# Two-layer Fourier, retention and attention trunk on one core: the Fourier projections use four banks in turn, and the last two tiles of the output projection take a shorter residual path

## The chip, the cores and the metric

One Trainium2 chip, one of its cores. The metric is the device time of one execution in microseconds, from runs of the whole program. Engines are named as in the profile: PE is TensorE, DVE VectorE, ACT ScalarE, POOL GpSimd, and SP SyncE, which here issues the DMAs.

## The reference

Two layers of a mixer over 1152 tokens of width 1024: 128 context tokens and 1024 latent tokens, modulated by two conditioning vectors. Cut to what matters here, one layer is:

```
h   = rms_norm(x, g_pre) * (1 + scale) + shift
fx, fz, rq, rk, rv, rz, aq, ak, av, az, mg = split_columns(h @ w_in)
ya  = (fourier_mix(fx) @ w_four) * silu(fz)          # real part of a 2-D DFT
yb  = rms_norm(bidir_retention(rope(rq), rope(rk), rv)) * silu(rz)
yc  = windowed_attention(rope(aq), rope(ak), av) * silu(az)
merged = ga * (ya @ w_pa) + gb * (yb @ w_pb) + gc * (yc @ w_pc)
x   = x + gate * rms_norm(merged @ w_out, g_post)
```

All of it is in float32. Outputs are x of the second layer and, for each layer, the new keys, values and retention states of the context tokens.

## The kernel before

The tokens lie in nine tiles of 128: tile 0 is the context, tiles 1 to 8 are latent. For products over token columns they are also taken as three chunks of 384. Each float32 operand is split into a high and a low half (`hi`, `lo`; for h the arrays `HH` and `HL`), and each product is three matrix multiplications: high by high, low by high, high by low. A weight is loaded to a tile `raw` (512 KB), cast to its high half by ACT (L174) and subtracted to its low half by POOL (L175).

PSUM has eight banks, given out by name: two `pj`, two `sl`, two `tr`, one `sc`, one `pv`. A projection needs a bank until its reader has copied the result out. `proj_t` (L218 to L220) multiplies eight blocks of a transposed weight with a chunk, 24 multiplications of 384 columns. `proj_n` (L228 to L230) multiplies a token tile with 512 columns, 24 multiplications as well.

In each layer the parts come in this order:

- a first group of natural projections (retention's keys and values), one tile at a time into a `pj` bank. Tile 0 is copied by ACT (L525) to `ns`; latent tiles go through the rotary step on DVE (L482 to L492) and a copy on ACT (L539). The rope table is loaded ahead of it (L508).
- the Fourier block. For each chunk it makes four projections into `acc` (L640). Of the first two ACT casts `XH` (L643) and DVE subtracts `XL` (L644); the other two go through a gate (ACT tanh L235, DVE L237). Then the group transforms (L651 to L653) into `sl`, copied by ACT to `Pn` (L654), a butterfly over the latent tiles on DVE (L673, L677, L681), and last the products with the DFT table (L717, L730). A second group of natural projections is mixed with the butterfly; its keys and values go through `kv` (ACT L537).
- retention, attention, gates and the branches' merge.
- the output projection (the loop from L1205). Each tile is multiplied with `w_out`, half into a `pj` bank and half into `sl`. ACT takes the sum of squares of each half (L1219), DVE and POOL make the reciprocal root (L246, L248), DVE scales both halves with it and with the gate (L1239), POOL adds the old x (L1242), and x is stored (L1246).
- in layer 0 each such tile at once becomes the next layer's h in `make_h` (L259): norm (ACT Square L254, DVE L246, POOL L248, DVE L256), eight transposes on PE (L268) into two `tr` banks, four affine steps on DVE for each bank (L272), the cast to `HH` on ACT (L277) and the subtraction to `HL` on DVE (L278).

The last tile of the last layer has its own way in the program before: the products with the gate are made first (L1226, L1229), so that after the reciprocal root only one step for each half remains (L1232), and there is no sum on POOL.

In the code tokens and engines are plain loops; a scheduler places every instruction on its engine with a model of time, and each engine then works its list in order. Tiles of a pool are reused when the last reader of the place is done. So the next layer's first group is mixed with the output projection's last tiles, and a change in one place moves instructions elsewhere. Constants of the next layer are also made there: decays and masks of retention (`la` to `lg`, `RD`, `WR`, `DD`, L570 to L609), the Fourier weight `MF` (PE L628, ACT L630), and slices of the next modulation (`macc`, L435 and L437).

Of the kernel before, what the change touches and what calls it, by code (L numbers as in the profile page):

```python
# [11 lines left out]
AF = mybir.ActivationFunctionType  # L12
# [4 lines left out]
P = 128  # L17
D = 1024
KT = 8
NT = 9  # L20
TOK = NT * P
CH = 384
# [60 lines left out]
def hybrid_step(ctx, tc, ins, cst, outs):  # L83
    nc = tc.nc
    PE, ACT, DVE, POOL, SP = nc.tensor, nc.scalar, nc.vector, nc.gpsimd, nc.sync
# [26 lines left out]
    x_d = dram("scr_x", (TOK, D))  # L112
# [17 lines left out]
    def pj(shape):  # L130
        return bank("pj", 2, shape)
# [17 lines left out]
    sh = mk(const, [P, KT, 2], "sh")  # L149
    sm = mk(const, [P, KT, 2], "sm")  # L150
    siluc = mk(const, [P, KT, 2], "siluc")
    shn = mk(const, [P, KT, 2], "shn")
    smn = mk(const, [P, KT, 2], "smn")
# [102 lines left out]
        DVE.tensor_scalar(xh, xt, r, None, op0=ALU.mult)  # L256
        return xh

    def make_h(pl, xt, t, sm, sh):  # L259

        s = 0 if t == 0 else 1
        xh = norm_x(pl, xt)
        tok = slice(t * P, (t + 1) * P)
        for half in range(2):
            pt = tr([P, 4, P])
            for kk in range(4):
                k = half * 4 + kk
                PE.transpose(pt[:, kk, :], xh[:, k * P : (k + 1) * P], ident)  # L268
            hf = mk(pl, [P, 4, P], "hf")
            for kk in range(4):  # L270
                k = half * 4 + kk
                DVE.tensor_scalar(  # L272
                    hf[:, kk, :], pt[:, kk, :], sm[:, k, s : s + 1], sh[:, k, s : s + 1],
                    op0=ALU.mult, op1=ALU.add,
                )
            ks = slice(half * 4, half * 4 + 4)
            ACT.copy(HH[:, ks, tok], hf)  # L277
            DVE.tensor_tensor(out=HL[:, ks, tok], in0=hf, in1=f(HH[:, ks, tok]), op=ALU.subtract)  # L278
# [216 lines left out]
    for l in range(DEPTH):  # L495
        last = l == DEPTH - 1
# [118 lines left out]
        with pool("fo", side="right") as fo:  # L615
            gz = mk(fo, [P, 2, TOK], "gz")
            Pn = mk(fo, [P, NT, 512], "Pn")
            with pool("xt", side="right") as xp:
                MFh = mk(xp, [P, 2, 512], "MFh", F32R)
                MFl = mk(xp, [P, 2, 512], "MFl", F32R)  # L620
                cdft = mk(xp, [P, 2, P], "cdft")
                SP.dma_start(cdft, cst["cdft"].rearrange("p (a b) -> p a b", a=2))
                w4 = mk(xp, [P, 2, 256], "w4")
                SP.dma_start(w4, ins["w_four"][l].rearrange("(k p) f -> p k f", p=P))
                for i in range(2):
                    mf = sl([P, 2, 256])
                    for r in range(2):
                        PE.matmul(mf[:, r, :], cdft[:, r, :], w4[:, i, :], start=True, stop=True)  # L628
                    mfv = MFh[:, i, :].rearrange("p (a b) -> p a b", a=2)
                    ACT.copy(mfv, mf)  # L630
                    DVE.tensor_tensor(
                        out=MFl[:, i, :].rearrange("p (a b) -> p a b", a=2), in0=mf, in1=f(mfv), op=ALU.subtract
                    )
                XH = mk(xp, [P, 2, TOK], "XH", F32R)
                XL = mk(xp, [P, 2, TOK], "XL", F32R)
                us = [unit_t(w_in, c0) for c0 in (C_FX, C_FX + P, C_FZ, C_FZ + P)]
                for c in range(NCH):
                    tok = slice(c * CH, (c + 1) * CH)
                    for i in range(4):
                        acc = pj([P, CH])  # L640
                        proj_t(us[i], c, acc)
                        if i < 2:
                            ACT.copy(XH[:, i, tok], acc)  # L643
                            DVE.tensor_tensor(out=XL[:, i, tok], in0=acc, in1=f(XH[:, i, tok]), op=ALU.subtract)  # L644
                        else:
                            gate_evac(fo, acc, gz[:, i - 2, tok])
                for t in range(NT):
                    tok = slice(t * P, (t + 1) * P)
                    acc = sl([P, 512])
                    for i in range(2):  # L650
                        PE.matmul(acc, XH[:, i, tok], MFh[:, i, :], start=(i == 0), stop=False)  # L651
                        PE.matmul(acc, XH[:, i, tok], MFl[:, i, :], start=False, stop=False)
                        PE.matmul(acc, XL[:, i, tok], MFh[:, i, :], start=False, stop=(i == 1))  # L653
                    ACT.copy(Pn[:, t, :], acc)  # L654
# [550 lines left out]
        for t in range(NT):  # L1205
# [14 lines left out]
                accs.append(acc)  # L1220
            s1 = mk(wo3, [P, 1], "s1", bufs=2)
            DVE.tensor_tensor(out=s1, in0=ss[:, 0:1], in1=ss[:, 1:2], op=ALU.add)
            end = last and t == NT - 1
            if end:
                xg = mk(wo3, [P, D], "xg")
                DVE.tensor_tensor(out=xg[:, 0:512], in0=accs[0], in1=gpb[:, s, 0:512], op=ALU.mult)  # L1226
# [1 line left out]
            if end:  # L1228
                DVE.tensor_tensor(out=xg[:, 512:D], in0=accs[1], in1=gpb[:, s, 512:D], op=ALU.mult)  # L1229
                for n in range(2):  # L1230
                    ns = slice(n * 512, n * 512 + 512)
                    DVE.scalar_tensor_tensor(  # L1232
                        out=xo[:, ns], in0=xg[:, ns], scalar=r, in1=xo[:, ns], op0=ALU.mult, op1=ALU.add
                    )
                    SP.dma_start(y_s[0, (t - 1) * P : t * P, ns], xo[:, ns])
                continue
            for n in range(2):
                ns = slice(n * 512, n * 512 + 512)
# [40 lines left out]
```

## Time and profile before

| what | value |
|---|---|
| median of 3 runs | 2003.23 us (2001.77 to 2006.81) |
| the profiled execution's own time | 2004.05 us |
| its span, first to last instruction | 2002.3 us |
| PE busy | 1961.0 us, 98% |
| DVE busy | 991.0 us, 49% |
| ACT busy | 678.1 us, 34% |
| POOL busy | 549.0 us, 27% |
| mean granted PE clock | 0.995 of full speed |

Busy time is summed over the span. PE's lead over the others is so large that the idle time of any other engine costs something only where PE waits for it; the list of PE's waits and the windows in which PE is busy for less than their length are the places to look at. The granted clock of 1.00 is 2.4 GHz, 0.50 is 1.2 GHz.

### The profile page before, as it was taken

What the parts mean: (1) busy time and instruction counts of PE and PEld (TensorE: products, weight loads), DVE (VectorE), ACT (ScalarE), POOL (GpSimd) and SP (SyncE); (2) the same over time, 40 slices, a digit from 0 to 9 for tenths busy, and PEclk for the clock granted to TensorE, in tenths of its full rate; (3) what the DMA queues carried; (4) which work ended last, traced back from release to release, by engine and by line L of the source; (5) the groups of instructions that cost most, each with busy time, mean ns of one, the idle gap of its engine ahead of it and who ended that gap; (6) DMA issues with size and microseconds to landing.
All of it is one profiled execution on the core that took longest, in us unless ns stands there. A gap on an engine that the chain in (4) does not pass through costs nothing.

```text
span 2002.3 us, 29865 instructions
## 1 busy us (share of the span) xinstructions
PE 1961.0 (98%) x11046; PEld 1794.2 (90%) x11046; DVE 991.0 (49%) x2557; ACT 678.1 (34%) x1536; POOL 549.0 (27%) x424
## 2 busy tenths in 40 slices
PE   8999999999999999999999999999999999999998
PEld 2898878999999999999878878899999999999987
DVE  4626556556667765104675272444556665410411
ACT  3522111234555444114331212022455555421411
POOL 2222232111112332444441214122111222333342
PEclk9999999999999999999999999999999999999999
DMA  9323554353334334323344145234422433422142
GB/s 298 105 72 98 149 139 135 102 178 105 97 116 123 117 103 137 91 89 128 116 135 101 58 103 162 74 115 129 125 82 88 121 100 97 143 92 83 60 153 85
DMA packets 245186, 230.53 MB, mean 115 GB/s; under 512 B 37920, under 2 KB 215856, under 8 KB 244784
## 3 DMA queue, kind: packets, MB, share of 16 engines
q1 hardware_dynamic: 245040, 228.62, 37.6%
q8 instruction: 87, 1.43, 0.3%
q14 instruction: 59, 0.48, 0.1%
HBM read 170.14 MB, written 58.42 MB: 114 GB/s over the span
## 4 chain that ended last, share of the span: by engine, by line
PE 88%; DMA 4%; DVE 3%; ACT 1%; issue 1%; SPq 1%; POOL 1%; DVEq 0%; POOLq 0%; ACTq 0%
PE pj L218 13%; PE pj L220 13%; PE pj L219 13%; PE pj L228 5%; PE pj L229 5%; PE pj L230 5%; PE tr L1102 3%; DMA raw<-in_w_in 2%; PE sl L1048 2%; PE pv L1109 2%; PE pv L1108 2%; PE sl L951 2%; PE sl L953 2%; PE sl L952 2%; PE pj L951 2%; PE pj L952 2%
## 5 line engine op out<-in xcount | busy, mean ns | idle before, releaser
L218 PE MATMUL pj<-HH,uh 128*128 128x384 f32 x1440 | 491.0, 341 | 9.0 <-DVE XL L644 4.2
L219 PE MATMUL pj<-HL,uh 128*128 128x384 f32 x1440 | 485.4, 337 | 0.0
L220 PE MATMUL pj<-HH,ul 128*128 128x384 f32 x1440 | 485.3, 337 | 0.0
L175 POOL TENSOR_TENSOR ul<-raw,uh 128x1024 fp32r<-128x1024 f32 x80 | 192.4, 2406 | 491.1 <-ACT uh L174 400.0
L218 PEld LDWEIGHTS pj<-HH,uh 128*128 128x128 f32 x1440 | 271.0, 188 | 14.2 <-ACT mth L948 4.9
L219 PEld LDWEIGHTS pj<-HL,uh 128*128 128x128 f32 x1440 | 271.2, 188 | 1.6
L220 PEld LDWEIGHTS pj<-HH,ul 128*128 128x128 f32 x1440 | 270.9, 188 | 1.5
L174 ACT CAST uh<-raw 128x1024 fp32r<-128x1024 f32 x80 | 84.0, 1049 | 172.3 <-PE pj L219 123.6
L437 DVE SCALAR_TENSOR_TENSOR macc<-mw,siluc,macc 128x256 f32<-128x256 f32 x224 | 134.7, 644 | 8.2 <-DMA mw<-in_w_mod 8.2
L228 PE MATMUL pj<-uh,HH 128*128 128x512 f32 x336 | 133.7, 399 | 3.7 <-ACT kv L537 1.8
L229 PE MATMUL pj<-ul,HH 128*128 128x512 f32 x336 | 132.8, 395 | 0.0
L230 PE MATMUL pj<-uh,HL 128*128 128x512 f32 x336 | 132.3, 394 | 0.0
L954 DVE SCALAR_TENSOR_TENSOR M<-M,sl 128x384 f32<-128x384 f32 x48 | 26.6, 554 | 202.2 <-PE sl L953 197.1
L1085 ACT ACTIVATE E<-E,NM 128x640 f32<-128x640 f32 (+1 forms) x128 | 101.9, 798 | 66.5 <-DVE NM L1081 66.4
L1106 DVE TENSOR_TENSOR El<-tr,Eh 128x512 fp32r<-128x512 f32 x132 | 89.0, 685 | 45.9 <-ACT Eh L1105 45.6
L1105 ACT CAST Eh<-tr 128x512 fp32r<-128x512 f32 x132 | 74.7, 587 | 86.8 <-PE tr L1102 85.1
L966 POOL TENSOR_TENSOR mth<-mth,ml 128x384 f32<-128x384 f32 x48 | 51.7, 1077 | 178.0 <-DVE mth L954 122.5
L1102 PE MATMUL tr<-ident,E 128*128 128x128 f32 x528 | 84.0, 272 | 0.2 <-ACT E L1085 0.2
L954 DVE SCALAR_TENSOR_TENSOR mth<-mth,pj 128x384 f32<-128x384 f32 x96 | 52.9, 551 | 63.1 <-ACT mth L948 31.9
L966 POOL TENSOR_TENSOR M<-M,mrow 128x384 f32<-128x384 f32 x48 | 48.7, 1015 | 123.1 <-DVE M L954 73.5
L1066 DVE CUSTOM_DVE_ANT_0 E<-sl,mask,m 128x384 f32<-128x384 f32 (+1 forms) x128 | 72.1, 579 | 17.4 <-PE sl L1048 17.0
L228 PEld LDWEIGHTS pj<-uh,HH 128*128 128x128 f32 x336 | 63.3, 188 | 19.2 <-ACT kv L537 1.9
(312 smaller groups left out, 4038.4 us busy)
## 6 DMA issues: line engine op xcount, KB each, us to landing
raw<-in_w_in SPq DMA_DIRECT2D x84, 512.0 KB
scr_m<-mth SPq DMA_DIRECT2D x96, 192.0 KB
mw<-in_w_mod SPq DMA_DIRECT2D x128, 128.0 KB
scr_n<-ns SPq DMA_DIRECT2D x36, 256.0 KB
ml<-scr_m SPq DMA_DIRECT2D x48, 192.0 KB
mrow<-scr_m SPq DMA_DIRECT2D x16, 576.0 KB
big<-in_w_mod SPq DMA_DIRECT2D x16, 512.0 KB
raw<-in_w_out SPq DMA_DIRECT2D x16, 512.0 KB
```

The source lines that it names most:

```text
L175: POOL.tensor_tensor(out=lo, in0=raw, in1=f(hi), op=ALU.subtract)
L218: PE.matmul(acc, hi[:, k, :], HH[:, k, tok], start=(k == 0), stop=False)
L219: PE.matmul(acc, hi[:, k, :], HL[:, k, tok], start=False, stop=False)
L220: i = PE.matmul(acc, lo[:, k, :], HH[:, k, tok], start=False, stop=(k == KT - 1))
L228: PE.matmul(acc, a, hi[:, k % 2, :], start=(k == 0), stop=False)
L229: PE.matmul(acc, a, lo[:, k % 2, :], start=False, stop=False)
L230: i = PE.matmul(acc, b, hi[:, k % 2, :], start=False, stop=(k == KT - 1))
L437: DVE.scalar_tensor_tensor(out=accs[s], in0=w, scalar=siluc[:, k, s : s + 1], in1=accs[s], op0=ALU.mult, op1=ALU.add,)
L966: POOL.tensor_tensor(out=th, in0=th, in1=ml, op=ALU.add)
L1085: ACT.activation(Es[hh][:, 0:nk], srcs[hh], AF.Exp, bias=NM[t][:, hs + hh : hs + hh + 1], scale=0.125, accum_out=DEN[t][:, hs + hh : hs + ...
L1102: PE.transpose(pt[:, hh, hp_, :], Es[2 * hp_ + hh][:, n * P : (n + 1) * P], ident)
L1106: DVE.tensor_tensor(out=El, in0=pt, in1=f(Eh), op=ALU.subtract)
```

## The change

There are three edits. The four projections of a chunk in the Fourier block take the banks `pj`, `sc`, `pj` and `pv` in turn, instead of the two `pj` alone. The path without POOL's sum is taken by tiles 7 and 8 in both layers, instead of tile 8 of the last layer alone; in layer 0 its end is the store of x and `make_h`. In that call of `make_h` the second and fourth affine step of each half are done by ACT instead of DVE.

```
-    def make_h(pl, xt, t, sm, sh):
+    def make_h(pl, xt, t, sm, sh, both=False):
...
             for kk in range(4):
                 k = half * 4 + kk
+                if both and kk % 2:
+                    ACT.activation(
+                        hf[:, kk, :], pt[:, kk, :], AF.Identity, bias=sh[:, k, s : s + 1], scale=sm[:, k, s : s + 1]
+                    )
+                    continue
                 DVE.tensor_scalar(
...
-                        acc = pj([P, CH])
+                        acc = (pj, sc, pj, pv)[i]([P, CH])
                         proj_t(us[i], c, acc)
...
-            end = last and t == NT - 1
+            end = t >= NT - 2
             if end:
                 xg = mk(wo3, [P, D], "xg")
...
-                    SP.dma_start(y_s[0, (t - 1) * P : t * P, ns], xo[:, ns])
+                    if last:
+                        SP.dma_start(y_s[0, (t - 1) * P : t * P, ns], xo[:, ns])
+                if not last:
+                    SP.dma_start(x_d[t * P : (t + 1) * P, :], xo)
+                    make_h(wo3, xo, t, smn, shn, True)
                 continue
```

Line numbers in the text are those of the kernel before; in the changed kernel those of the Fourier block stand 5 further on. The order changes at the Fourier block of each layer and at the turn between the layers. Three places follow, as each engine's list has them; a number behind a name is a buffer's.

ACT's list at the start of layer 1's Fourier block, before: `XH` are the casts of the first two projections, `gth` the gates of the other two, and the second weight cast is for a later stage.

```order
L174 CAST uh_10817<-raw_10815 128x1024
L643 CAST XH_10795<-pj_10821 128x384
L174 CAST uh_11262<-raw_11259 128x1024
L643 CAST XH_10795<-pj_10848 128x384
L235 ACTIVATE gth_10900<-pj_10875 128x384
L235 ACTIVATE gth_10934<-pj_10909 128x384
```

And with the change:

```order
L174 CAST uh_10821<-raw_10819 128x1024
L648 CAST XH_10799<-pj_10825 128x384
L174 CAST uh_11266<-raw_11263 128x1024
L648 CAST XH_10799<-sc_10852 128x384
L235 ACTIVATE gth_10904<-pj_10879 128x384
L235 ACTIVATE gth_10938<-pv_10913 128x384
```

The order on ACT is the same, with the same weight cast between the two `XH`; only the banks that are read differ.

ACT's list at the turn from layer 0 to layer 1, before: L277 are casts of tile 7's halves, L525 the copy of tile 0 of the next layer's first projection out of its bank, L254 tile 8's Square.

```order
L572 ACTIVATE lu_10724<-la_10722 128x8
L277 CAST HH_77<-hf_10166 128x4x128
L525 COPY ns_10357<-pj_10318 128x512
L254 ACTIVATE xh_10251,ss_10252<-xo_10185 128x1024
L174 CAST xh_10799<-raw_10797 128x1024
L277 CAST HH_77<-hf_10178 128x4x128
```

The end of the same stretch with the change, where L273 are ACT's affine steps, L282 the casts of tile 8's halves, L613 is the exponent of `DD` (L608 before), and L530 is the copy that was L525:

```order
L635 CAST MFh_10783<-sl_10789 128x512
L613 ACTIVATE DD_10764<-DD_10764 128x512
L273 ACTIVATE hf_10268<-tr_10263,shn_74,smn_75 128x128
L635 CAST MFh_10783<-sl_10794 128x512
L273 ACTIVATE hf_10268<-tr_10263,shn_74,smn_75 128x128
L282 CAST HH_77<-hf_10268 128x4x128
L273 ACTIVATE hf_10280<-tr_10275,shn_74,smn_75 128x128 x2
L282 CAST HH_77<-hf_10280 128x4x128
L530 COPY ns_10361<-pj_10322 128x512
```

The copy of tile 0 has moved from ahead of tile 8's Square to behind the last of tile 8's casts.

PE's list at tile 8's transposes, before: they stand within the third tile of the next layer's first projection (`pj_10401`).

```order
L228 MATMUL pj_10401<-uh_10308,HH_77 128x512
L229 MATMUL pj_10401<-ul_10309,HH_77 128x512
L230 MATMUL pj_10401<-uh_10308,HL_78 128x512
L268 MATMUL tr_10259<-ident_67,xh_10251 128x128 x4
L268 MATMUL tr_10271<-ident_67,xh_10251 128x128 x4
L228 MATMUL pj_10401<-uh_10308,HH_77 128x512
```

And with the change, where `pj_10364` is the second tile, `pj_10405` the third, and L633 the products of the Fourier weight (L628 before):

```order
L229 MATMUL pj_10364<-ul_10319,HH_77 128x512
L230 MATMUL pj_10364<-uh_10318,HL_78 128x512
L268 MATMUL tr_10263<-ident_67,xh_10255 128x128 x4
L633 MATMUL sl_10789<-w_2019_10787,cdft_10785 128x256 x2
L633 MATMUL sl_10794<-w_2019_10787,cdft_10785 128x256 x2
L268 MATMUL tr_10275<-ident_67,xh_10255 128x128 x4
L228 MATMUL pj_10405<-uh_10300,HH_77 128x512
```

The third tile, which reuses the bank of the first, now stands whole behind the transposes, and the Fourier weight's products stand between their halves.

## Rows read from the trace of the kernel before

**Rows 1.** The page, busy time of each engine with its share of the span and its count of instructions.

```profile
PE 1961.0 (98%) x11046; PEld 1794.2 (90%) x11046; DVE 991.0 (49%) x2557; ACT 678.1 (34%) x1536; POOL 549.0 (27%) x424
```

**Rows 2.** Waits of PE over the whole span: line that waited, what it waited for, microseconds in total, times, the longest.

```profile
PE pj L218 <- DVE XL L644: 4.2, 1, 4.2
PE pj L228 <- ACT kv L537: 3.7, 2, 2.0
...
PE tr L268 <- DVE xh L256: 1.7, 1, 1.7
...
PE pj L228 <- DVE xh L1239: 1.2, 1, 1.2
```

**Rows 3.** Windows: length, busy time of PE, PEld, DVE, ACT, POOL with counts, granted PE clock, DMA share, GB/s. The first is the stretch behind the waits at the turn between the layers, the other two the start after the Fourier wait.

```profile
1050.00:1060.00 10.00, 10.00 (x48) 8.33 (x47) 9.97 (x37) 2.72 (x8) 0.00 (x0) 1.00 0.35 109
...
1106.00:1108.00 2.00, 2.00 (x6) 2.00 (x7) 1.83 (x3) 0.00 (x0) 1.42 (x1) 0.50 0.01 4
1108.00:1110.00 2.00, 2.00 (x10) 2.00 (x10) 0.00 (x0) 0.00 (x0) 0.00 (x0) 0.73 0.61 194
```

**Rows 4.** Timeline of ACT in layer 1's Fourier block: start, duration (us), what ran, and in brackets the idle time before it and what ended it.

```profile
1103.88 1.04 ACT L174 CAST uh<-raw 128x1024 fp32r<-128x1024 f32 x1 [10.63 <-DMA raw<-in_w_in]
1104.83 0.47 ACT L643 CAST XH<-pj 128x384 fp32r<-128x384 f32 x1
```

**Rows 5.** Timeline of SP's DMA issues there.

```profile
1091.22 0.92 SPq L463 DMA_DIRECT2D scr_mod<-gtn  x2
1092.20 16.13 SPq L203 DMA_DIRECT2D raw<-in_w_in  x5
```

**Rows 6.** Timeline of PE there, the first multiplication after the wait and three at the end of the slow stretch.

```profile
1105.94 0.69 PE L218 MATMUL pj<-HH,uh 128*128 128x384 f32 x1 [4.16 <-DVE XL L644]
...
1109.23 0.34 PE L219 MATMUL pj<-HL,uh 128*128 128x384 f32 x1
1109.40 0.34 PE L220 MATMUL pj<-HH,ul 128*128 128x384 f32 x1
1109.58 0.34 PE L218 MATMUL pj<-HH,uh 128*128 128x384 f32 x1
```

**Rows 7.** Timeline of POOL at the turn between the layers: tile 8's sum and a weight's subtraction.

```profile
1038.83 2.39 POOL L1242 TENSOR_TENSOR xo<-xo,xh 128x1024 f32<-128x1024 f32 x1 [2.69 <-DVE ld L575]
...
1046.57 2.37 POOL L175 TENSOR_TENSOR xl<-raw,xh 128x1024 fp32r<-128x1024 f32 x1
```

**Rows 8.** Timeline of ACT there: the copy of tile 0, tile 8's Square, the exponent of `DD`, the cast of tile 8's second half.

```profile
1043.48 0.58 ACT L525 COPY ns<-pj 128x512 f32<-128x512 f32 x1
1043.96 1.06 ACT L254 ACTIVATE xh<-xo 128x1024 f32<-128x1024 f32 x1
...
1054.69 0.63 ACT L608 ACTIVATE DD<-DD 128x512 f32<-128x512 f32 x1 [2.80 <-DVE DD L604]
...
1061.09 0.62 ACT L277 CAST HH<-hf 128x512 fp32r<-128x512 f32 x1 [2.50 <-DVE hf L272]
```

**Rows 9.** Timeline of DVE there: tile 7's norm, the decay, four affine steps, four small operations, tile 8's norm, a split, and the steps of `DD`.

```profile
1033.66 0.74 DVE L256 TENSOR_SCALAR xh<-xo,hrr 128x1024 f32<-128x1024 f32 x1
...
1036.78 0.17 DVE L570 SCALAR_TENSOR_TENSOR la<-lx 128x8 f32<-128x8 f32 x1 [1.32 <-DMA lx<-in_ret_decay]
...
1041.56 1.36 DVE L272 TENSOR_SCALAR hf<-tr,smn,shn 128x128 f32<-128x128 f32 x4
1042.84 0.76 DVE L583 SCALAR_TENSOR_TENSOR lq<-lq,lz 128x8 f32<-128x8 f32 x4
...
1046.64 2.85 DVE L256 TENSOR_SCALAR xh<-xo,hrr 128x1024 f32<-128x1024 f32 x1 [0.18 <-POOL hrr L248]
1049.41 0.68 DVE L278 TENSOR_TENSOR HL<-hf,HH 128x512 fp32r<-128x512 f32 x1
...
1051.54 0.87 DVE L603 TENSOR_SCALAR DD<-rdf,lg 128x128 f32<-128x128 f32 x4
...
1053.79 0.87 DVE L604 SCALAR_TENSOR_TENSOR DD<-rdf,lg,DD 128x128 f32<-128x128 f32 x3
```

**Rows 10.** Timeline of PE there: the third tile's start, tile 8's transposes, and six of the eight products of the Fourier weight.

```profile
1044.11 0.50 PE L228 MATMUL pj<-uh,HH 128*128 128x512 f32 x1 [0.18 <-ACT ns L525]
...
1049.55 1.09 PE L268 MATMUL tr<-ident,xh 128*128 128x128 f32 x8 [1.66 <-DVE xh L256]
...
1058.10 1.46 PE L628 MATMUL sl<-w,cdft 128*128 128x256 f32 x6
```

**Rows 11.** Timeline of DVE at the end of the last layer: tile 8's last step there, both halves.

```profile
1997.72 1.41 DVE L1232 SCALAR_TENSOR_TENSOR xo<-xg,xrr,xo 128x512 f32<-128x512 f32 x2 [0.73 <-POOL xrr L248]
```

**Rows 12.** Timeline of POOL there: tile 7's sum.

```profile
1987.91 2.39 POOL L1242 TENSOR_TENSOR xo<-xo,xh 128x1024 f32<-128x1024 f32 x1 [1.58 <-DVE xh L1239]
```

**Rows 13.** Timeline of PE in the second half of layer 1's Fourier block: the last two multiplications of the group transforms, and the first products of latent tiles with the DFT table.

```profile
1164.09 0.39 PE L652 MATMUL sl<-MFl,XH 128*128 128x512 f32 x1
1164.32 0.40 PE L653 MATMUL sl<-MFh,XL 128*128 128x512 f32 x1
...
1191.26 1.50 PE L730 MATMUL pv<-dft,SD 128*128 128x128 f32 x12
```

**Rows 14.** Timeline of DVE there: the start and the end of the butterfly.

```profile
1165.38 2.29 DVE L673 TENSOR_TENSOR SD<-Pn 128x2048 f32<-128x2048 f32 x1 [10.70 <-ACT Pn L654]
...
1187.16 2.80 DVE L681 SCALAR_TENSOR_TENSOR SD<-Pn 128x512 f32<-128x512 f32 x6
```

## The prediction

> **What bounds the kernel now.** First the page: TensorE is busy for 1961.0 of the span's 2002.3 us [rows 1]. The change alters no matrix multiplication, so it can win only from the 41 us in which TensorE stands, and from multiplications that ran at the low clock. Second, TensorE's list of waits tells where these lie [rows 2]. Two belong to the lines of the change: one wait of 4.2 us for `XL` (L644) in a Fourier block, and at the turn from layer 0 to layer 1 1.7 us for L256's `xh` and 1.2 us for L1239's `xh`, with 0.18 us for L525's copy [rows 10] some 3.0 us together. Third, the windows show how long TensorE worked and which clock it was granted [rows 3]: after the 1.7 us wait the clock stayed at 1.00, after the 4.2 us wait it fell to 0.50. Fourth, the timelines around the two places give the durations [rows 4 to 14].
>
> **Fourier banks, layer 1: 5.7 us gained.** ACT casts the second `XH` at 1104.83 only since ahead of it in ACT's order stands a weight cast, for a later stage, whose load came at 1103.88 [rows 4]. That load was issued behind the store of `scr_mod` at 1091.22 [rows 5]. The two banks of `pj` are then held by the second and third projection, and the fourth waits: TensorE stands for 4.16 us until 1105.94 [rows 6]. In the new order the same cast still stands between the two `XH` casts, but the second projection lies in `sc`, the third in the other `pj` bank, the fourth in `pv`, and the first projection of the next chunk finds its `pj` bank free. So TensorE can do two projections more (24 products each, at the 0.173 us between starts that rows 6 show at the end) before it needs what ACT holds back: 2 x 24 x 0.173 = 8.3 us of cover for a wait of 4.2. The wait goes. With it goes the low clock behind it: ten intervals from 1105.94 to 1109.23 took 3.29 us where ten of 0.173 take 1.73, so 1.56 us. Sum 4.16 + 1.56 = **5.7 us**. Late next would be the second projection of the next chunk, which needs `sc`; it comes 8.3 us later and finds it free by 4.1 us. In layer 0 the list of waits has no such entry, so nothing is gained there.
>
> **Fourier, second half: 0.** With four banks the order puts all twelve projections ahead of the group transforms (L651 to L653), which before were mixed with them. By the order listing the last transform comes 29 TensorE rows later, about 6.7 us at the 0.23 us between starts [rows 13]. VectorE's butterfly starts on it: it took from 1165.38 to the end of L681 at 1189.96, 24.6 us [rows 14], and TensorE came to L730 at 1191.26 [rows 13]. The first large group that needs the butterfly now stands 109 TensorE rows behind the last transform, 25.3 us, so it is met within a microsecond. The wait for L537's copies, 3.7 us in two [rows 2], I leave as it is. Bounds: it goes (-3.7), or doubles (+3.7).
>
> **The turn between the layers: 5.8 us lost.** Removed for tile 8 is POOL's sum of 2.39 us [rows 7], which holds the chain to the transposes, and the `pj` bank comes free with L1226 instead of after rstd. But the listings show two other moves. The copy of the next layer's first tile (L525), at 1043.48 ahead of tile 8's Square before [rows 8], now stands last, behind every cast of tile 8 and behind the exponent of `DD` (L608). And tile 8's transposes stand after two tiles of the next projection, with L628's products between their halves, and the third tile, which takes the bank that this copy empties, comes right behind. So I follow TensorE and the copy.
>
> *TensorE.* It began the third tile at 1044.11 [rows 10]; without the 0.18 and the 1.20 us of waits it has done two tiles and tile 7 at 1042.7. Tile 8's chain: the decay load at 1036.78 still stands ahead [rows 9]; three small operations and one affine step to 1037.5; L1232 1.41 [rows 11]; Square 1.06, with its sum some 1.2 [rows 8]; POOL's power 0.73 as in the tail [rows 11], with the small steps before it 0.9; L256 0.74 [rows 9]: 1041.7. So the transposes don't wait. They take 1.09 and L628's eight products, six of which took 1.46, 1.95 [rows 10]: TensorE is done at 1045.8.
>
> *The copy.* VectorE must first do, from 1041.7: about twelve small operations (0.15 each, by the four in 0.76), two splits of 0.68, two affine steps of 0.34, the four RD and WR as small ones, 0.6, then L603 0.87 and four of L604, about 1.2 [rows 9]: 1.8 + 1.36 + 0.68 + 0.6 + 0.87 + 1.2 = 6.5, less 0.4 of small operations that end behind it. That is 1047.8. On ACT then `DD`'s exponent 0.63 [rows 8], the alternating affine steps of the first half behind L609 (some 1.5), a cast of 0.62, a split and the second half's four (some 1.4), a cast of 0.62 and the copy 0.58 [rows 8]: 5.3, so **1053**. TensorE stands from 1045.8 to 1053, 7.2 us, where it stood for 3.04: +4.2. After a wait of 7 us I take the clock's dip as after 4.2 us, +1.6. Sum **+5.8**.
>
> Bounds: if nothing but tile 8's own casts is in front of the copy, it comes 1.9 us after the transposes (0.7 for four steps, 0.62, 0.58): 3.04 becomes 1.9, -1.1 with no dip. If the exponent of `DD` ends no earlier than it did (it started at 1054.69), the copy ends 5.3 us behind that, at 1060.0, TensorE stands for 14.2, +11.2, with the dip +12.8. I take the value nearer to the lower end, since by the listing rotary steps and L437, which stood on VectorE ahead of that exponent, now stand behind it.
>
> L256 took 2.85 us beside POOL's subtract at 1046.57 (2.37 us), against 0.74 alone [rows 7, 9]. The Trainium skill, page "SBUF — State Buffer", section "Who interferes with whom", says that GpSimd and VectorE share one pair of ports as an exclusive lock, so that such an operation waits out the other's whole instruction, and that an operation with two SBUF inputs meets it too; L1232 has two where L1239 has one. The trace agrees with the lock; by it, with a bad start of L256, the loss here would be 7.9 instead of 5.8. I don't take that, as in the new order the raw weight's cast stands behind tile 8's Square and its subtract comes later than L256. A second rule speaks against the alternation in `make_h`: page "PSUM — Partial Sum Buffer", section "PSUM bank collisions raise a hardware error", has two engines on one bank kept apart by dependencies, so ACT and VectorE would take turns on a half's bank and save nothing. No row shows such a pair; with it the sum is the one above, without it some 0.6 us per half better.
>
> Also moved: the load of the rope table, issued before the output projection so far, now stands behind the last store of it, since `xg` takes its room. It must be there when the second tile's bank is wanted, 5.5 us (24 x 0.23) after the copy; I cost it at nothing.
>
> **The tail: 0.** Tile 8 of layer 1 had the new form before [rows 11]. Tile 7's POOL sum there (1987.91, 2.39 us) [rows 12] lay beside tile 8's products and its removal frees nobody.
>
> **Sum.** The profiled execution took 2004.05 us (span 2002.3), 0.8 over the median of the runs. 2004.05 - 5.7 + 5.8 + 0 + 0 = 2004.15; at the level of the median **2003.3 us**. About 0.3%, 6 us, is what a measurement of this kernel tells from no change: 1997.2 to 2009.2.
>
> **Rivals.**
> A, faster: the turn goes as the edit has it. The copy ends by 1047.7 since the exponent of `DD` is ready early, TensorE stands for 1.9 us and keeps its clock. For it: POOL's sum is gone from tile 8's chain. Against it: the 6.1 us of VectorE work in front. 2003.2 - 5.7 - 1.1 = 1996.4. The wait for L537 going as well would give 1993.
>
> B, slower: the copy, last in ACT's order, is bound to `DD`, whose chain starts at loads (decay at 1036.78) that come no earlier, and ends where it ended before. Copy at 1060.0: 2003.2 - 5.7 + 12.8 = 2010.3; with L537's wait doubled in one layer 2012.1. It decides from a copy at about 1058.9 on.
>
> C, the banks do nothing: the late load still stops TensorE, because `pv` or `sc` is held by something else, and the 4.2 us only move to another projection. For it: ACT's order there is the same as before. Against it: 8.3 us of cover. 2003.2 + 5.8 = 2009.0.
>
> **How the numbers follow.** The forecast has 0.46, A 0.26, B 0.20, C 0.08. Forecast and most of C are within 0.3%: 0.52. A is faster: 0.26. B and the rest of C: 0.22 slower. The range reaches to A's value, its lower variant left out, and past B's: 1996 to 2011.
>
> **What would show it.** Fourier: no wait of TensorE on L644's successor, granted clock 1.00 where it was 0.50. Turn: one TensorE wait of some 7 us for ACT's copy of the first tile's `ns` just behind tile 8's transposes, none for L1239, and a stretch at low clock behind it. Wrong would be: no wait there (A), one above 13 us (B), a wait on `XL` that remains (C), or new waits on L730 or L537 above 4 us in all. The tail ends as before.

## The result: 2015.4 us, 0.67% slower, and the profile after

The changed kernel takes 2015.39 us (median of 4 runs, 2014.95 to 2015.85), the kernel before 2002.5 us (median of 4; the 2003.23 us further up is that of the first three). The ratio is 1.0067, with an interval of 1.0048 to 1.0086. The prediction was 2003.3 us with a range to 2011. The profiled execution took 2015.69 us (span 2013.9), 11.6 us more than that of before.

TensorE's waits over the whole span come first, with the columns of [rows 2]: line that waited, what for, total, times, longest. In the changed kernel L530 was L525, L542 was L537, L782 was L777.

```profile
PE pj L228 <- ACT ns L530: 10.7, 1, 10.7
PE tr L313 <- DVE hrv L246: 8.1, 1, 8.1
PE tr L782 <- POOL vw L773: 5.1, 2, 2.8
PE pj L228 <- ACT kv L542: 4.2, 2, 2.1
PE pj L218 <- ACT kv L542: 3.5, 1, 3.5
...
PE tr L268 <- DVE lq L588: 1.5, 1, 1.5
PE tr L268 <- ACT hf L273: 1.5, 1, 1.5
```

The first line is the wait that the prediction named, for the copy of the first tile. The wait for `XL`, 4.2 us in [rows 2], is gone. The wait of 3.5 us for L542 before a transposed projection (layer 0) was 0.4 us; the list of before has it as

```profile
PE pj L218 <- ACT kv L537: 0.4, 1, 0.4
```

The windows, with the columns of [rows 3]: three across the turn between the layers, one at the place of the old Fourier wait.

```profile
1040.00:1050.00 10.00, 4.18 (x22) 2.86 (x20) 7.79 (x30) 5.43 (x13) 2.90 (x2) 0.93 0.69 212
1050.00:1060.00 10.00, 2.03 (x5) 1.65 (x6) 7.51 (x20) 4.92 (x10) 0.00 (x0) 0.50 0.35 106
1060.00:1070.00 10.00, 10.00 (x41) 8.06 (x40) 3.76 (x11) 0.38 (x1) 0.00 (x0) 0.89 0.31 98
1100.00:1110.00 10.00, 10.00 (x61) 10.00 (x59) 2.85 (x7) 1.90 (x3) 3.52 (x2) 1.00 0.69 137
```

At the turn TensorE works for 6.2 of 20 us, and from 1050 to 1060, within the long wait and behind it, its granted clock is 0.50. In the Fourier block it works without a gap at 1.00, where [rows 3] had 0.50.

TensorE's three waits at the turn, in its timeline. They answer to [rows 10].

```profile
1042.71 0.63 PE L268 MATMUL tr<-ident,xh 128*128 128x128 f32 x4 [1.55 <-DVE lq L588]
...
1046.62 0.66 PE L268 MATMUL tr<-ident,xh 128*128 128x128 f32 x4 [1.55 <-ACT hf L273]
...
1057.97 0.79 PE L228 MATMUL pj<-uh,HH 128*128 128x512 f32 x1 [10.70 <-ACT ns L530]
```

Together they are 13.8 us, where the waits of before made 3.0. The list puts the first one down to L588, a small operation; what these transposes read is tile 8's norm, which ends at 1042.56. ACT there, against [rows 8]: a weight cast that waits for its load, the affine step behind it, the exponent of `DD`, a step of tile 8's second half, the copy.

```profile
1044.22 1.04 ACT L174 CAST xh<-raw 128x1024 fp32r<-128x1024 f32 x1 [2.33 <-DMA raw<-in_w_in]
...
1046.10 0.46 ACT L273 ACTIVATE hf<-tr,shn,smn 128x128 f32<-128x128 f32 x1 [0.48 <-DVE hf L277]
...
1051.10 0.63 ACT L613 ACTIVATE DD<-DD 128x512 f32<-128x512 f32 x1 [1.41 <-DVE DD L609]
...
1055.39 0.46 ACT L273 ACTIVATE hf<-tr,shn,smn 128x128 f32<-128x128 f32 x1 [1.34 <-DVE hf L277]
...
1057.34 0.58 ACT L530 COPY ns<-pj 128x512 f32<-128x512 f32 x1
```

And VectorE, against [rows 9]: tile 7's last step of the new path, the first step of the decay, tile 8's norm, an affine step that waits for ACT's, a small operation beside POOL's subtract, and the start of `DD`.

```profile
1020.57 4.93 DVE L1237 SCALAR_TENSOR_TENSOR xo<-xg,xrr,xo 128x512 f32<-128x512 f32 x2
...
1037.70 0.17 DVE L575 SCALAR_TENSOR_TENSOR la<-lx 128x8 f32<-128x8 f32 x1 [0.92 <-DMA lx<-in_ret_decay]
...
1041.81 0.75 DVE L256 TENSOR_SCALAR xh<-xo,hrr 128x1024 f32<-128x1024 f32 x1 [0.25 <-POOL hrr L248]
...
1045.66 0.41 DVE L277 TENSOR_SCALAR hf<-tr,smn,shn 128x128 f32<-128x128 f32 x1 [1.42 <-ACT hf L273]
1045.98 1.73 DVE L589 SCALAR_TENSOR_TENSOR lq<-lq,ls 128x8 f32<-128x8 f32 x1
...
1048.48 0.87 DVE L608 TENSOR_SCALAR DD<-rdf,lg 128x128 f32<-128x128 f32 x4
```

POOL's subtract there:

```profile
1045.34 2.35 POOL L175 TENSOR_TENSOR xl<-raw,xh 128x1024 fp32r<-128x1024 f32 x1 [3.56 <-ACT xh L174]
```

Tile 8's norm starts at 1041.81 and ends at 1042.56, predicted was 1041.7. The exponent of `DD` starts at 1051.10, predicted was 1047.8; the copy ends at 1057.92, predicted was 1053. ACT's two `XH` casts in layer 1's Fourier block, against [rows 4]: the late weight still stands between them.

```profile
1103.96 0.48 ACT L648 CAST XH<-pj 128x384 fp32r<-128x384 f32 x1
1114.43 1.05 ACT L174 CAST uh<-raw 128x1024 fp32r<-128x1024 f32 x1 [9.99 <-DMA raw<-in_w_in]
1115.39 0.47 ACT L648 CAST XH<-sc 128x384 fp32r<-128x384 f32 x1
```

**Where the 11.6 us are.** At instructions that hold the same place in both programs, one can read by how much TensorE of the changed kernel is late against the other trace:

| from | to | lateness changes by |
|---|---|---|
| start | layer 0's Fourier block | +0.5 us |
| there | retention of layer 0 | +2.2 |
| there | output projection of layer 0 | -4.2 |
| there | layer 1's Fourier block (the turn) | +12.7 |
| there | retention of layer 1 | -2.6 |
| there | the end | +3.0 |

The turn is 10.8 us of standing (13.8 against 3.0) and 1.9 us of low clock. In layer 1's Fourier block the first half gives 5.7 us and the second takes back 3.1. Of the parts outside the change (-4.2 and +3.0) single places can be named: the wait for `gth` at 340 us was 1.8 us with a granted clock of 0.50 behind it and is 1.0 us with a clock of 1.00 now; the other way, the clock is 0.51 from 1247 to 1250 now, where it was 1.00. The two programs do the same work there; that these differences are not the change's is likely, but no run shows it.

### The profile page after: what moved, and what is told of

The parts are those of the page before. It is cut to its first block, busy times and chain, and to the rows that moved or that the text cites. A ratio compares the mean times of both kernels' runs of the same rounds, so it can differ in the third digit from the quotient of the medians.

```text
span 2013.9 us, 29872 instructions
## 1 busy us (share of the span) xinstructions
PE 1962.1 (97%) x11046; PEld 1796.1 (89%) x11046; DVE 994.3 (49%) x2555; ACT 682.5 (34%) x1544; POOL 548.6 (27%) x421
## 4 chain that ended last, share of the span: by engine, by line
PE 88%; DMA 4%; DVE 4%; ACT 2%; issue 1%; SPq 1%; POOL 1%; DVEq 0%; POOLq 0%; ACTq 0%
PE pj L218 13%; PE pj L220 12%; PE pj L219 12%; PE pj L228 5%; PE pj L229 5%; PE pj L230 5%; PE tr L1107 3%; PE sl L1053 2%; PE pv L1114 2%; PE pv L1113 2%; PE sl L956 2%; PE sl L958 2%; PE sl L957 2%; PE pj L956 2%; PE sl L229 2%; PE sl L230 2%
## 5 line engine op out<-in xcount | busy, mean ns | idle before, releaser
L218 PE MATMUL pj<-HH,uh 128*128 128x384 f32 x1344 | 460.5, 343 | 7.9 <-ACT kv L542 3.5
L219 PE MATMUL pj<-HL,uh 128*128 128x384 f32 x1344 | 454.5, 338 | 0.0
L220 PE MATMUL pj<-HH,ul 128*128 128x384 f32 x1344 | 454.0, 338 | 0.0
L218 PEld LDWEIGHTS pj<-HH,uh 128*128 128x128 f32 x1344 | 254.1, 189 | 12.2 <-ACT mth L953 4.7
L219 PEld LDWEIGHTS pj<-HL,uh 128*128 128x128 f32 x1344 | 254.2, 189 | 1.5
L220 PEld LDWEIGHTS pj<-HH,ul 128*128 128x128 f32 x1344 | 253.8, 189 | 1.5
L228 PE MATMUL pj<-uh,HH 128*128 128x512 f32 x336 | 133.8, 399 | 13.3 <-ACT ns L530 10.7
L174 ACT CAST uh<-raw 128x1024 fp32r<-128x1024 f32 x80 | 84.0, 1050 | 176.2 <-PE pj L219 116.3
```

The costliest lines, as they stand in the source:

```text
L218: PE.matmul(acc, hi[:, k, :], HH[:, k, tok], start=(k == 0), stop=False)
L219: PE.matmul(acc, hi[:, k, :], HL[:, k, tok], start=False, stop=False)
L220: i = PE.matmul(acc, lo[:, k, :], HH[:, k, tok], start=False, stop=(k == KT - 1))
L228: PE.matmul(acc, a, hi[:, k % 2, :], start=(k == 0), stop=False)
```

## The experiments

Times of before differ between chips, from 1993.9 to 2007.2 us, so each kernel is compared with before on its own chip. e1 to e4 ran on one chip, e5 to e8, e9 to e12 and e13 to e16 on three others. The theories and rivals in the expectations have letters of their own: their rivals A and B are not those of the prediction.

### First: which part of the change costs, and by what

**e1, the banks without the turn** (the short path for tile 7 of the last layer only).

```
-            end = t >= NT - 2
+            end = last and t >= NT - 2
```

> The four banks and the shorter path for tile 7 of the last layer alone; layer 0 keeps the old path. Theory M (the loss lies at the turn between the layers, and there in the place of xg): the 10.7 us wait of TensorE for the copy of the next layer's first tile is absent, the 4.2 us wait of layer 1's Fourier block is absent too, the second halves of the Fourier blocks give back some 3 us in layer 1 and about 1 us in layer 0; time 1999 to 2002 us, 1 to 3 us under before. Rival B (the banks themselves cost, since all projections stand ahead of the group transforms): 2005 us or more.

Measured: 2003.05 us against 2007.17, ratio 0.9982 (0.9971 to 0.9993). No wait for L530 over 0.5 us and none for `XL`. So the banks gain some 4 us on this chip, and the loss lies elsewhere.

**e2, the turn without the banks.**

```
-                        acc = (pj, sc, pj, pv)[i]([P, CH])
+                        acc = pj([P, CH])
```

> The new path of tiles 7 and 8 in both layers, Fourier banks as before. Theory M: the turn costs some 13 us whatever the Fourier block does, and layer 1's 4.2 us wait is back: 2015 to 2018 us, TensorE waits of 10 to 11 us for the first tile's copy. Rival B: 2006 us or less.

Measured: 2021.87 us, ratio 1.0067 (1.0043 to 1.0091), with the wait of 10.7 us for L530 and that of 3.8 us for `XL`. The time is above the expected band, since before too was slower on this chip; the 13.4 us that the ratio makes fit theory M. Rival B falls.

**e3, the whole change without the alternation.**

```
-                    make_h(wo3, xo, t, smn, shn, True)
+                    make_h(wo3, xo, t, smn, shn)
```

> The whole change, but all four affine steps of each half stay on VectorE. Rival A (the alternation of ACT and VectorE on a half makes tile 8's casts and with them the copy late): the copy comes 5 us or more earlier, 2007 to 2010 us. Theory M: the listing still has the copy behind all casts of tile 8 and the exponent of DD; without the hops it ends 1 to 3 us earlier than 1057.9, TensorE waits 8 to 10 us for it, 2012 to 2015 us.

Measured: 2017.48 us, ratio 1.0046 (1.0028 to 1.0064). ACT's copy in e3's timeline:

```profile
1058.56 0.58 ACT L530 COPY ns<-pj 128x512 f32<-128x512 f32 x1
```

It starts no earlier than in the change. TensorE waits 7.1 us for it instead of 10.7, but 5.7 us for tile 8's norm ahead of it. Rival A falls: without the alternation the copy is late all the same. Theory M missed too, as it had the copy 1 to 3 us earlier: VectorE's list is another one here, with the norm, at 1049.28, behind a split that waited for ACT. So e3 does not tell what the alternation itself costs.

**e4, the whole change with `xg` in the squares' tile.** The squares written there are not read again, only their sums.

```
-                xg = mk(wo3, [P, D], "xg")
+                xg = xn
```

> The whole change, but xg is written over the tile that the squares were written to, so it takes no room of its own. By the listing the rope table's load stands ahead of the output projection again and the first tile's copy ahead of tile 8's second-half casts and of DD's exponent. Theory M: TensorE's wait for that copy falls to under 3 us, the clock dip goes, 2000 to 2004 us, 11 to 15 us under the change. Rival A (alternation) or a rival that blames the two-SBUF-input steps beside POOL: 2010 us or more, since both are still there.

Measured: 2005.36 us, ratio 0.9986 (0.9973 to 0.9999). ACT's copy and the exponent, in e4's timeline:

```profile
1040.88 0.58 ACT L530 COPY ns<-pj 128x512 f32<-128x512 f32 x1
...
1050.76 0.63 ACT L613 ACTIVATE DD<-DD 128x512 f32<-128x512 f32 x1 [1.89 <-DVE DD L609]
```

And TensorE's waits at e4's turn:

```profile
PE tr L268 <- DVE lq L588: 2.3, 1, 2.3
PE pj L228 <- ACT ns L544: 0.5, 1, 0.5
PE tr L268 <- ACT hf L273: 0.4, 1, 0.4
```

The exponent is as late as in the change, but the copy no longer stands behind it: it runs 16 us earlier, and the waits sum to 3.2 us. The path, the alternation and the steps with two SBUF inputs are all still there. What cost was the place of the copy, and that comes with the tile of its own that `xg` has, 4 KB in each partition. e4 also gives `xg` one of two places that are used in turn, where its own tile has one; no run keeps that apart from the room.

### Second: how the room of `xg` acts, and the banks' second half

**e5, e4 with the banks in the first chunk only.**

```
-                        acc = (pj, sc, pj, pv)[i]([P, CH])
+                        acc = ((pj, sc, pj, pv)[i] if c == 0 else pj)([P, CH])
```

> xg written over the squares' tile as in e4, and the four banks for the first of the three chunks only; chunks two and three use the two pj banks as before. Theory F (the banks' gain lies in the first chunk, their cost in putting the group transforms and the butterfly behind all twelve projections): layer 1's 4.2 us wait stays away, the last group transform comes 2 to 4 us earlier than in e4, and of L537's waits, 9.8 us in the profile of e4, 2 to 5 us go; 0 to 4 us under e4, ratio to before 0.996 to 0.999. Rival (the cost of the second half is not from the order): same as e4, ratio 0.9986.

Measured: 2024.07 us, ratio 1.0084 (1.0071 to 1.0098), far from both. TensorE's waits in e5:

```profile
PE pj L228 <- ACT kv L542: 16.6, 2, 8.4
...
PE pv L735 <- DVE gz L740: 5.4, 1, 5.4
PE pj L218 <- DVE grz L237: 4.2, 2, 3.8
```

Theory F falls: in layer 0 the last transform starts 3.1 us earlier than in e4, but VectorE's butterfly takes 29.0 us instead of 24.2, and nothing is given back. The waits shown sum to 26.2 us, where those of e4 for the same lines make 11.8. The longest are those for the `kv` copies, which wait for an earlier tile's store to free the place (`kv` has two). In layer 1 this is ACT's line and SP's order ahead of it:

```profile
1198.94 0.27 ACT L542 COPY kv<-pj 128x128 f32<-128x128 f32 x1 [7.96 <-DMA scr_n<-kv]
```

```profile
1185.92 0.89 SPq L468 DMA_DIRECT2D scr_mod<-gtn  x2
1186.90 0.42 SPq L552 DMA_DIRECT2D scr_n<-ns  x1
1189.91 0.33 SPq L553 DMA_DIRECT2D scr_n<-kv  x1
```

The stores of `scr_mod`, in single elements of 4 bytes, stand right ahead of the store that is waited for. In e4 they stand at 1161.46, and its waits for L542 in this stretch are 2.2 us. That made a further theory, tried below.

**e6, e4 with the rope table late.** The load is put behind the last store of the output projection in SP's order.

```
         if l:
+          with tc.issue_after(last_x[0]):
             SP.dma_start(ropet, cst["rope"].rearrange("(t p) f -> p t f", p=P))
...
-                    SP.dma_start(x_d[t * P : (t + 1) * P, :], xo)
+                    last_x[0] = SP.dma_start(x_d[t * P : (t + 1) * P, :], xo).ins
```

> e4 with the rope table's load put behind the last store of the output projection in SP's order, as it stands in the change, but without a conflict of room; by the listing the first tile's copy keeps its early place. Theory M (the copy's place costs, not the table's late arrival): no wait of TensorE over 3 us at the turn, within 2 us of e4, ratio 0.998 to 1.000. Rival R (the table itself comes too late): TensorE waits 4 us or more for a rotary step or an L539 copy, ratio 1.002 or more.

Measured: 2006.88 us, ratio 1.0000 (0.9988 to 1.0012); the waits at the turn are 1.9, 1.7 and 0.5 us, none for a rotary step. The late table costs nothing that can be told, and by itself it does not move the copy. So the copy's place comes with `xg`'s own tile, not from the load's order.

**e7, the change with other banks for the third and fourth tile.**

```
-                acc = pj([P, 8, 64])
+                acc = (sc if l and c0 == 0 and t == 2 else pv if l and c0 == 0 and t == 3 else pj)([P, 8, 64])
```

> The change with xg in its own room, but the third and fourth tile of layer 1's first projection use sc and pv, so that the third does not wait for the first tile's copy. By the listing the copy still stands last on ACT. Theory M (that copy holds TensorE only through its bank): the 10.7 us wait goes; the fifth tile needs the bank some 11 us later, about when the copy comes; waits at the turn 1 to 5 us in all, no long low clock, 8 to 13 us under the change, ratio 0.998 to 1.002. Rival (tile 8's transposes or the late rope table hold TensorE as well): 5 us or less under the change.

Measured: 2009.46 us, ratio 1.0006 (0.9991 to 1.0021). ACT's copy in e7's timeline, and TensorE's waits at its turn:

```profile
1057.60 0.58 ACT L530 COPY ns<-pj 128x512 f32<-128x512 f32 x1
```

```profile
PE tr L268 <- ACT hf L273: 2.3, 1, 2.3
PE tr L268 <- DVE lq L588: 1.7, 1, 1.7
```

The copy is as late as in the change (1057.34), nobody waits for it, and the granted clock is 1.00 from 1040 to 1070. By the ratios this is 12 us under the change. This shows the last link: the late copy held TensorE through its bank alone.

**e8, the turn by itself with `xg` in the squares' tile** (e4 with the banks of e2).

> The new path of tiles 7 and 8 in both layers with xg over the squares' tile, Fourier banks as before. Theory M: the turn costs TensorE about the 3 us that it cost before the change, so this edit by itself is worth -2 to +2 us, and layer 1's 4 us Fourier wait is back: ratio 0.999 to 1.001. Rival (the shorter chain does gain): 0.998 or less.

Measured: 2003.33 us, ratio 0.998 (0.9968 to 0.9992). It is the lowest ratio of all runs; with e1 and e4 it is one of three versions whose interval lies below the kernel before. By the ratio it is in the rival's band, but the waits at the turn sum to 4.2 us in its profile, no less than before the change, so the shorter chain is not where it gains. The wait for `XL` is 1.0 us. In e8 one weight load more stands ahead of the `scr_mod` store; the late weight came 9.6 us behind the cast before it, against 12.5 in the trace of before.

### Third: the late loads

**e9 and e10 to e12: the stores of `scr_mod` issued by ACT**, in the kernel before (e9), in e4 (e10), e5 (e11) and e8 (e12).

```
                 for s in range(2):
-                    SP.dma_start(
+                    ACT.dma_start(
                         mod_d[l, s, c0 - 2 * D : c0 - 2 * D + 256].rearrange("(k p) -> p k", p=P), dst[:, :, s]
```

> The kernel before the change, with the stores of scr_mod (256 single elements of 4 bytes each, L463) issued by ACT instead of SP. Theory S (transfers issued on SP's queue behind such a store land some 10 us later, and this made the weight late that stopped layer 1's Fourier block): the late weight cast comes before the second XH is due, TensorE's 4.2 us wait goes without any change of banks, L537's waits shrink too: 4 to 9 us under before, ratio 0.9955 to 0.998. Rival Q (the transfers themselves, not the queue, are slowed, or ACT's issue costs as much): ratio 0.999 or more, the wait stays.

> e4 (the change with xg over the squares' tile) with ACT's stores of scr_mod. Theory S: L542's waits, 9.8 us in three in e4's profile, fall under 5 us: ratio to before 0.995 to 0.998. Rival Q: 0.9986 as e4.

> e5 (banks in the first chunk only, 1.0084) with ACT's stores of scr_mod. Theory S (e5 lost since a store of scr_mod stands right ahead of the kv stores that TensorE waits for: issued at 1185.92, kv's copy free at 1198.94): the 16.6 us of L542 waits fall under 6 us, ratio 0.996 to 1.000. Rival (e5's loss is from its order alone): ratio 1.005 or more.

> e8 (new path at the turn, xg over the squares' tile, Fourier banks as before) with ACT's stores of scr_mod. Theory S: layer 1's Fourier wait goes or stays under 1 us, L542's shrink: ratio 0.9945 to 0.997, the fastest of all. Rival Q: 0.998 as e8.

Measured on one chip, where before took 1993.87 us:

| kernel | median us | ratio to before |
|---|---|---|
| e9 | 1994.08 | 0.9994 (0.9985 to 1.0003) |
| e10 | 2003.19 | 1.0045 (1.0032 to 1.0058) |
| e11 | 2018.85 | 1.0123 (1.0109 to 1.0136) |
| e12 | 1993.03 | 0.9994 (0.9984 to 1.0004) |

All four missed theory S by the ratio. e9 and e12, which differ by the new path of the last two tiles alone, have the same ratio: without the late store that path gains nothing. e9 has no wait for `XL` in its profile, yet it is no faster than before on this chip; whether before has that wait there is not known, since no trace of it was taken. e11 keeps 12.5 us of waits for L542 (16.6 in e5) with the store moved away: most of e5's loss is therefore not from that store. And both kernels with the new banks (e10, e11) are slower than before here. e10 differs from e12 by the four banks alone, on the same chip: 10.2 us more, with intervals that lie far apart. TensorE's waits for the `kv` copies in e10, and below them in e12:

```profile
PE pj L228 <- ACT kv L542: 4.2, 2, 2.1
PE pj L218 <- ACT kv L542: 3.9, 1, 3.9
```

```profile
PE pj L228 <- ACT kv L542: 1.2, 1, 1.2
```

So where the late weight is early enough, the four banks by themselves cost, 10 us here; in the two profiles these waits differ by 6.9 us.

**e13 to e16: two by two on one more chip**, with a trace of before on it. e13 is before once more, e14 has the edit of e9, e15 is e1 again, e16 is e15 with that edit.

> The program before the change, once more, for its trace on the same chip as the next three. Theory S (layer 1's Fourier wait comes from the load behind the scr_mod store and varies with the chip's transfers): ratio 1.000; on a chip with a time near 1994 us the wait for XL is under 2 us, on one near 2005 us it is 3 to 5 us.

> Before, with ACT's stores of scr_mod, on the same chip as e13. Theory S: if e13 has the XL wait, it is gone here and the time is 3 to 8 us less; if e13 has none, the same time within 2 us. Rival Q (the queue does not matter): the wait stays whatever e13 shows.

> The four banks alone (with tile 7's short path in the last layer), the stores on SP. Theory F2 (the banks take the 4 us wait where there is one and cost some 4 us in the second halves by waits for L542's copies anywhere): ratio to before 0.998 to 0.999 if e13 has the wait, 1.001 to 1.004 if not.

> The four banks and ACT's stores of scr_mod. Theory F2: since the wait is gone already, the banks only cost: 2 to 6 us over e14, with waits for L542 of 4 us or more in all where e14 has under 3. Rival: the same as e14 within 1 us.

| stores of `scr_mod` by | old banks | new banks |
|---|---|---|
| SP | 2008.45 us, 1.0010 (e13) | 2005.51 us, 0.9993 (e15) |
| ACT | 2003.67 us, 0.9988 (e14) | 2008.15 us, 1.0003 (e16) |

The intervals reach 0.10 to 0.17% to either side, so only the differences along a row or column of about 0.2% speak, and weakly. In e13 the late weight is cast here, with a wait of 3.5 us for `XL` behind it:

```profile
1091.38 1.05 ACT L174 CAST uh<-raw 128x1024 fp32r<-128x1024 f32 x1 [2.21 <-DMA raw<-in_w_in]
1102.84 1.04 ACT L174 CAST uh<-raw 128x1024 fp32r<-128x1024 f32 x1 [9.99 <-DMA raw<-in_w_in]
```

In e14 it comes 8.8 us behind the cast before it instead of 11.5, and the wait is 0.4 us:

```profile
1086.14 1.05 ACT L174 CAST uh<-raw 128x1024 fp32r<-128x1024 f32 x1 [2.08 <-DMA raw<-in_w_in]
1094.93 1.05 ACT L174 CAST uh<-raw 128x1024 fp32r<-128x1024 f32 x1 [7.20 <-DMA raw<-in_w_in]
```

So the store has a part in the wait. The weight comes in two loads of 256 KB, and in e13 the stores stand between them; the second load is the one that ends the wait. SP's issues in e13:

```profile
1091.29 0.46 SPq L463 DMA_DIRECT2D scr_mod<-gtn  x1
1091.80 0.46 SPq L203 DMA_DIRECT2D raw<-in_w_in  x1
```

And the second load in e14:

```profile
1085.65 0.77 SPq L203 DMA_DIRECT2D raw<-in_w_in  x1
```

In e13 it is issued 0.4 us behind the start of the cast before, in e14 0.5 us ahead of it; from the issue to the late cast it takes 11.0 us and 9.3 us. So of the 2.7 us between the two traces 0.9 us is a later issue and 1.8 us a slower arrival, and most of the delay stays with the store moved away. With the wait all but gone, the banks cost: e16 is 4.5 us over e14, and its waits for L542 are 7.5 us where e14 has 4.8 (under 3 was expected). That is theory F2, on this chip at the edge of what the runs can tell, and clear in e10 against e12.

## Why the prediction was wrong, step by step

- **Fourier, first half (-5.7 us): right.** The wait for `XL` and the low clock behind it are gone in the profile after, with ACT's order unchanged, as the step had it. The runs add a limit: the gain exists only where the weight is late. In e13 the wait is 3.5 us, in e8 1.0, in e14 0.4, in e9 none. And the cover has an end: in e7 the late weight is cast 13.4 us behind the cast before it, and TensorE waits 1.3 us before a projection that needs `sc`, the place that the prediction named as next.
- **Fourier, second half (0): wrong, some 5 us too low.** Lateness grew by 2.2 us over layer 0's block and by 3.1 us over the second half of layer 1's. The step was "the wait for L537's copies I leave as it is". In the trace these waits went from 3.7 us in two and 0.4 us in one to 4.2 and 3.5; 1.4 us for `grz` in layer 1 is new, and 1.7 us for it in layer 0 is gone. These make 3.3 of the 5.3 us; the rest is not traced to a wait. Its own bound (doubled, +3.7) was near that and was left out of the sum. e1, e15 and e16 keep such waits (8.9, 10.5 and 7.5 us), and e10 against e12 shows that they come with the banks. Which transfer sets them is not settled: e5's store theory explained the smaller part.
- **The turn (+5.8 us): the mechanism right, the size wrong by 6.9.** It measured +12.7. This step failed, in the time of the copy, and in its sum three terms. Tile 8's norm was to end at 1041.7; it ended at 1042.56, 0.9 us later, since the decay's load let its first step start at 1037.70 instead of 1036.78. VectorE's work from there to `DD`'s exponent was taken as 6.1 us; it was 8.5, with 1.42 us of waiting for ACT's alternate step, which stood behind a weight cast that waited for its load until 1044.22, and 1.6 us more for L589. And the last stretch on ACT was taken as 5.3 us; it was 6.8. There the split and the second half's four steps took 2.8 us instead of 1.4, with 1.34 and 0.48 us of waiting for VectorE's alternate steps. So the copy ended 4.9 us later than forecast. Another 1.5 us came since TensorE reached the transposes at 1041.2 instead of 1042.7: what it had gained ahead of the turn it stood for here, as the copy's chain starts at a load. That the transposes don't wait was wrong too (twice 1.55 us), but these waits add nothing, since TensorE would have stood as much longer for the copy. The sum took the steps of two alternating engines back to back, without their waits for each other.
- **Its bound.** The upper end, +12.8, is all but the measured +12.7, but its mechanism, rival B's, came true only in part. The chain did start at a load that came no earlier (1037.70 against 1036.78). Yet the exponent was not as late as before, 1051.10 against 1054.69, and the copy ended at 1057.92, ahead of the 1058.9 that B wanted; TensorE stood from earlier on. That the two figures meet is luck. B was given 0.20, against 0.46 for the value between.
- **The rope table (0): right in its price, wrong in what it was a sign of.** e6 shows that its late load costs nothing. But `xg`'s own tile, which moved it, moved the copy as well, as e4 shows; the prediction named the room and the copy's move in separate sentences and did not ask whether the one made the other. How the scheduler comes from that tile to the copy's place was not settled. Only the listings show it, and a late load alone (e6) does not do it.
- **The lock of POOL and VectorE.** L589, a small operation of 0.15 us, took 1.73 us beside POOL's subtract of 2.35 us at 1045.34, and tile 7's last step, two of 0.7 us, took 4.93 us beside two subtracts from 1019.74 on. This agrees with the Trainium skill, page "SBUF — State Buffer", section "Who interferes with whom". L256 was not hit (0.75 us), as the prediction had it, but L589 was, on the same chain.
- **Turns on one bank.** The alternation showed ACT and VectorE waiting for each other, as the page "PSUM — Partial Sum Buffer" of the Trainium skill, section "PSUM bank collisions raise a hardware error", would have it. But they also write one tile, `hf`, and no run parts the tile from the bank. Taking the alternation away (e3) left the copy late.
- **The clock (+1.6 us): right.** The turn's 12.7 us less 10.8 us of standing leave 1.9 us for multiplications at 0.50 behind the long wait.
- **The tail (0): right.** The span's end shows no new wait, and no run tells of a gain from tile 7 there.
- **Rival A** did not come from the change as written. e4 and e8 (0.9986 and 0.998 of before) lie between it and the forecast, but not by its mechanism: the waits at the turn are 3.2 and 4.2 us there, so the shorter chain still takes none of the standing away. **Rival C** fell.

The range missed since it took the turn's upper bound and the second half's upper bound one at a time. Both came in together: 5.3 us of second halves and 6.9 us of the turn beyond its forecast. The other differences, +0.5, -4.2 and +3.0, nearly cancel.

## What to carry to other kernels

A scratch tile is not free when it only fits: ask whose room it takes in the next stage, and look in the listing for what has moved before pricing the arithmetic of the edit. Here a tile of 4 KB in each partition cost 13 us through a copy that nobody had touched, and writing over a dead tile gave them back. Where a copy that empties a bank moves behind other work on its engine, follow the bank to the next one who wants it, and count every wait between engines that alternate, not their durations alone. And a projection that need not wait for its bank only reaches the next wait sooner: the four banks took away a wait of 4 us where a weight was late, and cost 10 us on a chip where it was not (e10 against e12).

## What the runs showed of the hardware

The same program took 1993.9 us on one chip and 2007.2 us on others, 0.7%, more than most edits tried here; what differs was not traced on each. Two stores of 256 single elements each, 1 KB each, went with a delay beyond their size: with them on SP between the two 256 KB loads of a weight, the second load took 11.0 us from its issue to the cast and was issued 0.9 us later against the cast before (e13); with ACT issuing them it took 9.3 us (e14). A small operation of VectorE with two inputs in SBUF took 1.73 us instead of 0.15 beside a subtract of POOL.
